# A chunkwise mLSTM and two feed-forward layers on one core: one merged state-update matmul, a sample chunk computed side by side, and five changes of order

## The chip, the cores and the metric

The kernel runs on one NeuronCore of a Trainium2 chip. Its engines are TensorE (PE in the profile; PEld is its weight load), VectorE (DVE), ScalarE (ACT), GpSimd (POOL) and SyncE (SP, which here issues nearly all DMAs). The metric is the device time of one execution in microseconds; "the time" of a kernel is the median of its runs.

## The reference, cut to what matters

The program is one inference step of a two-layer encoder for a prompt of 1024 frames and a sample of 32 frames, all in float32. Layer 0 is an mLSTM mixer, layer 1 a sliding-window attention with sinks; each is followed by a SwiGLU feed-forward part, and every sub-layer by `x <- LayerNorm(alpha * x + sublayer(x))`. So there are four LayerNorms; the kernel numbers them li = 0 (after the mLSTM), 1 (after the first feed-forward part), 2 (after the attention) and 3 (after the second).

The part that the change touches most is the recurrence over chunks of the mLSTM, per head with key size 64 and value size 128:

```
def mlstm_chunk(q, k, v, ig, lf, C0, n0, m0):
    b = jnp.cumsum(lf, axis=-1)
    log_d = where(causal, b[..., :, None] - b[..., None, :] + ig[..., None, :], -inf)
    inter = b + m0[..., None]
    m = jnp.maximum(inter, jnp.max(log_d, -1))
    d = jnp.exp(log_d - m[..., None])
    w_inter = jnp.exp(inter - m)
    qk = jnp.einsum('bhtd,bhsd->bhts', q, k) * d
    num = w_inter[..., None] * jnp.einsum('bhtd,bhde->bhte', q, C0) + jnp.einsum('bhts,bhse->bhte', qk, v)
    den = w_inter * jnp.einsum('bhtd,bhd->bht', q, n0) + jnp.sum(qk, -1)
    h = num / jnp.maximum(jnp.abs(den), jnp.exp(-m))[..., None]
    w_end = jnp.exp(b[..., -1:] - b + ig - m_new[..., None])
    C_new = decay[..., None, None] * C0 + jnp.einsum('bhs,bhsd,bhse->bhde', w_end, k, v)
    n_new = decay[..., None] * n0 + jnp.einsum('bhs,bhsd->bhd', w_end, k)
    return h, C_new, n_new, m_new
```

The final states `C` and `n` of the prompt and of the sample are outputs.

## The kernel before, in words

Activations lie transposed, features on the partitions and 1056 columns of time (1024 prompt, 32 sample). Dense products are made of three matmuls per 128 features of the contraction: each float32 operand is split into a high part in a reduced-precision float32 format and a low remainder, and `gemm` (lines 346 to 361; its matmuls are L358, L359, L360) adds high times high, high times low and low times high. Weights arrive by DMA (L157) and are split by ScalarE (the high part, L198) and by GpSimd or VectorE (the low part, L200).

Order is written out by hand. The dense products are the main thread; everything else is a Python generator in a `Weave`, and after each step of a product `wv.tick(us)` lets the generators whose pause is over emit their next instructions. A `yield 0.8` is thus a pause of 0.8 us of TensorE's dense work. `wv.drain(task)` emits the rest of a task at once. Every engine carries out its own instructions in the order in which they were emitted.

The stages on which the change bears:

- The mixer's projections, per pair of heads j (four pairs): `proj_q`, `proj_k` (heads on the output partitions) and `proj_v` (time on the output partitions, nine chunks of time: eight of 128 and the sample's of 32). For j = 0 `proj_v` makes the 16 gate columns too.
- `gate_task` and `gates(g)`: for three groups of columns, the gate arithmetic on 8 partitions; `gate_columns` transposes the result to time on the partitions (L786) and copies it to SBUF (L787). At the end one small product (L798) gives the decay of every chunk. It must be done before `begin()`, which starts the recurrence.
- `mlstm`: 36 visits (j, c), four pairs of heads by nine chunks, in five stages, one visit apart: `fetch` (DMAs of the decay rows, L824 and L828), `pre` (GpSimd, L839 to L846, and the exponentials L849 on ScalarE), `scores` (L856, L858), `values` (L872 to L916) and `place` (L923 to L925). In `values`, line 877 makes the state update of the two heads: two matmuls with 64 columns of weights each, one to PSUM partitions 0 to 63, one to 64 to 127. Line 890 adds it to the decayed state. After the last chunk of the prompt (c = 7) and after the sample's (c = 8) the state goes out by two DMAs, L897 and L898, the latter of one column of 128 values.
- `mixer_out` and the second half of `ffn` run over four quarters of 264 columns. After each quarter `norm_tail` launches an `ln_task`: a matmul with a constant matrix gives the mean (L417), VectorE centres (L422), ScalarE squares (L424), VectorE and GpSimd add the squares up (L426, L429), a second matmul gives the variance (L433), and the rest normalises (L438 to L469). Its pauses are the tuple `LN_PACE`. The matmul L433 stands in TensorE's stream between the matmuls of the next dense product.
- `ffn` begins while the fourth quarter's `ln_task` still runs: the first two up-projection tiles are plain products (`up_plain`), for half c = 0 of the columns and then for c = 1, and beside each half `sums(c)` makes the sums and differences of operands (L1240 to L1259) that the later tiles (`up_tile`, a scheme with seven products in place of eight) read.

Of the kernel before, what the change touches and what calls it, by code (L numbers as in the profile page):

```python
# [10 lines left out]
F32R = mybir.dt.float32r  # L11
# [41 lines left out]
    ((4.0, 1.2, 1.0, 3.6, 1.0, 1.4, 0.9), (3.8, 0.7, 0.8, 4.2, 0.8, 1.4, 1.0)),  # L53
    ((4.2, 0.9, 1.1, 4.4, 1.0, 1.4, 0.8), (4.2, 0.7, 0.9, 4.2, 0.8, 1.4, 0.8)),
)

RUSH = (3.2, 0.8, 0.6, 2.8, 0.8, 1.0, 0.6)

# [180 lines left out]
def kernel(ctx: ExitStack, tc: tile.TileContext, A, O):  # L239
# [14 lines left out]
    def new(p, tag, shape, dt=F32, bufs=1):  # L254
        uid[0] += 1
        return p.tile(list(shape), dt, name=f"{tag}_{uid[0]}", tag=tag, bufs=bufs)
# [106 lines left out]
    def psbank():  # L363
        return new(psx[1][0], "d", [P, 512], F32, bufs=psx[1][1])
# [30 lines left out]

    QUARTERS = [(group(g), (g % 2, slice(0, N4))) for g in range(4)]

    def ln_task(z_, lps, grp, li, last, final):
        cols, (c, zs) = grp
        w = cols.stop - cols.start  # L400

        rush = final and grp is QUARTERS[2]
        y = RUSH if rush else LN_PACE[li & 1][last]
        acc = z_[:, 0:2, c, zs]
        sq = [acc] + [z_[:, 2 + 2 * i : 4 + 2 * i, c, zs] for i in range(3)]
        rs, r2 = z_[:, 8, c, zs], z_[:, 9, c, zs]
        n = KT // 2

        def z2(kk):
            return ACT[:, 2 * kk : 2 * kk + 2, cols]  # L410

        def s2(i, kk):
            return SX[:, i, 2 * kk : 2 * kk + 2, cols]

        yield y[0]
        pm = new(lps, "ln", [P, 512], bufs=3 if li & 1 else 2)[:, :w]
        nc.tensor.matmul(pm, onesm[:], acc[:, 0, :], start=True, stop=True)  # L417
        yield y[1]
        for s in range(n + 2):
            if s < n:  # L420

                nc.vector.tensor_sub(z2(s), pm.unsqueeze(1).broadcast_to([P, 2, w]), z2(s))  # L422
            if 1 <= s <= n:
                nc.scalar.activation(sq[s - 1], z2(s - 1), AF.Square)  # L424
            if s >= 3:
                (nc.gpsimd if rush or not (last or s & 1) else nc.vector).tensor_add(acc, acc, sq[s - 2])  # L426
            yield y[2]
        if not rush:
            nc.vector.tensor_add(acc[:, 0], acc[:, 0], acc[:, 1])  # L429
        yield y[3]  # L430
        pv = new(lps, "ln", [P, 512], bufs=3 if li & 1 else 2)[:, :w]
        for i in range(1 + rush):
            nc.tensor.matmul(pv, onesm[:], acc[:, i, :], start=(i == 0), stop=(i == rush))  # L433
        yield y[4]

        if not li & 1:
            nc.scalar.preload_act_table_set("natural_log_exp_and_others")
        nc.scalar.activation(rs, pv, AF.Ln, bias=eps_ln[:])  # L438
        nc.scalar.activation(rs, rs, AF.Exp, scale=-0.5)
        nc.scalar.activation(r2, rs, AF.Square, scale=0.5 ** 0.5)  # L440
        yield y[5]
        nc.vector.scalar_tensor_tensor(r2, pv, eps_ln[:], r2, op0=ALU.add, op1=ALU.mult)
        nc.vector.scalar_tensor_tensor(rs, r2, 1.5, rs, op0=ALU.subtract, op1=ALU.mult)
        for s in range(n + 3):
            if s < n:
                eng = nc.gpsimd if rush and s & 1 else nc.vector
                eng.tensor_mul(z2(s), z2(s), rs.unsqueeze(1).broadcast_to([P, 2, w]))  # L447
            kk = s - 1
            if 0 <= kk < n:
                for k in (2 * kk, 2 * kk + 1):  # L450
                    z, gk, bk = ACT[:, k, cols], lng[:, li, k : k + 1], lnb[:, li, k : k + 1]
                    if rush and k & 1:
                        nc.gpsimd.tensor_scalar(z, z, gk, bk, op0=ALU.mult, op1=ALU.add)
                    elif li & 1 and last and k & 1:
                        nc.vector.tensor_scalar(z, z, gk, bk, op0=ALU.mult, op1=ALU.add)
                    else:
                        nc.scalar.activation(z, z, AF.Identity, scale=gk, bias=bk)  # L457
            kk = s - 2
            if 0 <= kk < n:
                if final:  # L460
                    nc.sync.dma_start(O["y"][:, 2 * kk : 2 * kk + 2, cols], z2(kk))
                else:
                    nc.scalar.copy(s2(0, kk), z2(kk))
                    if li == 1:
                        nc.scalar.dma_start(scr[:, 2 * kk : 2 * kk + 2, cols], z2(kk))
            kk = s - 3
            if kk >= 0 and not final:
                eng = nc.gpsimd if kk & 1 else nc.vector
                eng.tensor_sub(s2(1, kk), z2(kk), s2(0, kk).bitcast(F32))  # L469
            yield y[6]  # L470
# [216 lines left out]
    def proj_v(j):  # L687

        ua, ub = U_V[j]
        parts = [W.get(ua), W.get(ub)]  # L690
        m = 256 if j else 256 + NG
        rhs = []
        for k in range(KT):
            hi, lo = parts[k // 4][k % 4 // 2]
            s = slice((k % 2) * m, (k % 2) * m + m)
            rhs.append((hi[:, s], lo[:, s]))
        for c, c0, L, g, off in CH:
            ps = psbank()[:L, :m]
            gemm(ps, [(sxh[k][g][:, off : off + L], sxl[k][g][:, off : off + L]) for k in range(KT)], rhs)
            nc.vector.tensor_copy(vt[j][:L, c, :, 0:DV], ps[:, :256].rearrange("p (h e) -> p h e", h=2))  # L700
            if j == 0:
                nc.vector.tensor_copy(gt[:L, c, :], ps[:, 256:])
            mst["v"] += 1
        W.done(ua)
        W.done(ub)

    def gates(g):
# [40 lines left out]
            )  # L748
        yield 1.0
        if late:  # L750
            gate_columns(*late.pop())
        gg = g3[0:8, :n]
        nc.vector.tensor_sub(gg, ig, b)
        nm = b
# [27 lines left out]
    def gate_columns(g, g3):  # L782
        for c, c0, L, cg, off in CH:
            if cg == g:
                pt = new(psa, "T", [P, 512], bufs=2)
                nc.tensor.transpose(pt[:L, :96], g3[:96, off : off + L], ident[:96, :96])  # L786
                nc.scalar.copy(cols[g][:L, c % 3, :], pt[:L, :96])  # L787

    def gate_task():
        for g in range(3):  # L790
            while mst["v"] < 3 * g + 3:
                yield 0.5
            yield from gates(g)
        yield 3.0
        gate_columns(*late.pop())
        pd = new(psa, "T", [P, 512], bufs=2)
        for j in range(PAIRS):
            nc.tensor.matmul(pd[:, 9 * j : 9 * j + 9], sel[:, j, :], dec[:], start=True, stop=True)  # L798
        nc.vector.tensor_copy(dcol[:], pd[:, : 9 * PAIRS].rearrange("p (j c) -> p j c", j=PAIRS))

    mst = {"ready": 0, "done": 0, "v": 0, "go": False}
    prev = None
# [8 lines left out]
    def mlstm(gap):  # L811
# [53 lines left out]
        def values(j, c):  # L865
# [5 lines left out]
            for h in range(2):  # L871
                nc.tensor.matmul(ph[:L, h, :], s["p"][:L, h, :L], vt[j][:L, c, h, :], start=True, stop=C is None)  # L872
                if C is not None:
                    nc.tensor.matmul(ph[:L, h, :], s["qw"][:, h, :L], C[:], start=False, stop=True)
            for h in range(2):
                r = slice(64 * h, 64 * h + 64)
                nc.tensor.matmul(pc[r, : DV + 1], s["k"][:L, h, :], vt[j][:L, c, h, :], start=True, stop=True)

            small = new(pa2, "small", [P, 5, 2], bufs=3)
            enm = cols[g][:L, c % 3, 64 + 2 * j : 66 + 2 * j]  # L880
# [3 lines left out]
            nc.vector.scalar_tensor_tensor(u, den, -1.0, u, op0=ALU.mult, op1=ALU.max)  # L884
            nc.vector.reciprocal(u, u)
            Cn = new(pa2, "Cn", [P, DV + 1], bufs=3)
            if C is None:
                nc.vector.tensor_copy(Cn[:], pc[:, : DV + 1])
            else:
                nc.vector.scalar_tensor_tensor(  # L890
                    Cn[:], C[:], dcol[:, j, c : c + 1], pc[:, : DV + 1], op0=ALU.mult, op1=ALU.add
                )
            if c < 7:
                state[j, c + 1] = Cn
            else:
                k = "p" if c == 7 else "s"
                nc.sync.dma_start(O[k + "_C"][2 * DK * j : 2 * DK * (j + 1), :], Cn[:, :DV])  # L897
                nc.sync.dma_start(O[k + "_n"][2 * DK * j : 2 * DK * (j + 1), :], Cn[:, DV : DV + 1])  # L898
            junk = new(pa2, "junk", [P, DV])
            for h in range(2):  # L900
                nc.scalar.activation(
# [16 lines left out]
        def place(j, c):  # L918
            _, c0, L, g, off = CH[c]
            s = S.pop((j, c))  # L920
            pt = new(psa, "T", [P, 512], bufs=2)
            for h in range(2):
                nc.tensor.transpose(pt[:, h * P : h * P + L], s["h"][:L, h, :], ident[:L, :L])  # L923
            nc.scalar.copy(act[2 * j][g][:, off : off + L], pt[:, :L])
            nc.vector.tensor_copy(act[2 * j + 1][g][:, off : off + L], pt[:, P : P + L])  # L925

        def first(j, c):
            if c == 0:
# [189 lines left out]
    def ffn(layer, li, tasks, lx, final):  # L1118
# [107 lines left out]
        def sums(c):  # L1226
# [4 lines left out]

            todo = [(o, k) for k in range(0, H, 2) for o in ("t3", "t2", "t4")] + [("t1", k) for k in range(0, H, 2)]
            bufs = [Z[:, i : i + 2, c, :] for i in (7, 9)]

            def halve(s, low):
                if 0 <= s < len(todo):
# [675 lines left out]
```

## Time and profile before

| | |
|---|---|
| median of 3 runs | 2274.51 us (2273.16 to 2274.54) |
| profiled execution, own time | 2275.5 us |
| its span, first to last instruction | 2273.4 us |
| mean granted TensorE clock | 0.990 |
| TensorE busy | 2202.4 us, 97% of the span |
| VectorE busy | 1473.6 us, 65% |
| ScalarE busy | 1014.6 us, 45% |
| GpSimd busy | 1131.4 us, 50% |

How to read it: a group row gives line, engine, operation, the tiles written and read, the shapes and the count, then the busy time, the mean duration of one in ns, and the idle time of the engine just before them with what ended it. Matmuls overlap one another, so the duration of one (some 0.28 us) is not what it costs; the cost is the distance from its start to the next start. A float32 matmul without the split shows as two instructions. A row of waits gives the waiting instruction, the work that it waited for, the total in us, the number of times and the longest. A timeline row gives start and duration, and in brackets the engine's idle time just before and what ended it. A row of windows gives, for a stretch of time, each engine's busy time and instructions and the granted clock of TensorE (PEclk, 1.00 is full).

### The profile page before, as it was taken

How to read it: one execution, taken by the hardware profiler on the slowest of the kernel's cores; microseconds unless marked ns; L12 is line 12 of the kernel's file. 1: busy time of each engine (PE TensorE's matmuls, PEld its weight loads, DVE VectorE, ACT ScalarE, POOL GpSimd, SP SyncE). 2: the span in 40 equal slices, each digit the busy share in tenths (PEclk: the TensorE clock that was granted, in tenths of full speed). 3: DMA queues.
4: the chain of work that ended last, by engine and by line, in shares of the span. 5: the costliest groups of instructions: out<-in, count | busy, mean ns of one | idle time of the engine just before them, and what ended most of it. 6: DMA issues, size and time to landing. Idle time of an engine off the chain costs nothing. (4 is left out here: it accounts for less than half of the span.)

```text
span 2273.4 us, 44324 instructions
## 1 busy us (share of the span) xinstructions
PE 2202.4 (97%) x17190; PEld 2158.1 (95%) x17190; DVE 1473.6 (65%) x2771; ACT 1014.6 (45%) x2281; POOL 1131.4 (50%) x1040
## 2 busy tenths in 40 slices
PE   9999999999999999999998999989999999999997
PEld 9889989999999999999998998889999999999997
DVE  4354466777666665466667788877666666466657
ACT  4343354455444444322246788756444444432124
POOL 2443333226666665554326676633666666554422
PEclk9999999999999999999999999999999999999999
DMA  4222112301444444697424211311343344397712
GB/s 147 70 56 62 46 42 74 115 28 67 147 148 152 152 140 145 214 331 235 163 78 137 85 59 44 125 65 56 114 151 134 142 152 154 125 336 259 247 57 77
DMA packets 167394, 291.54 MB, mean 128 GB/s; under 512 B 16592, under 2 KB 123144, under 8 KB 167184
## 3 DMA queue, kind: packets, MB, share of 16 engines
q1 hardware_dynamic: 162832, 284.38, 37.1%
q10 hardware_dynamic: 4352, 4.33, 0.5%
q8 instruction: 135, 2.21, 0.4%
q14 instruction: 75, 0.61, 0.1%
HBM read 203.89 MB, written 82.94 MB: 126 GB/s over the span
## 5 line engine op out<-in xcount | busy, mean ns | idle before, releaser
L200 POOL TENSOR_TENSOR wl_s<-wr,wh_s 128x512 fp32r<-128x512 f32 x224 | 316.2, 1431 | 238.5 <-ACT wh_s L198 163.3
L358 PE MATMUL d<-sx,wh 128*128 128x264 f32 (+2 forms) x1068 | 342.4, 321 | 0.7 <-DVE act L1471 0.7
L360 PE MATMUL d<-sx,wl 128*128 128x264 f32 (+2 forms) x1068 | 328.4, 308 | 3.0 <-DVE wl L200 2.1
L359 PE MATMUL d<-sx,wh 128*128 128x264 f32 (+2 forms) x1068 | 328.1, 307 | 0.5 <-DVE sx L389 0.3
L198 ACT CAST wh_s<-wr 128x512 fp32r<-128x512 f32 x224 | 135.5, 617 | 317.4 <-DVE wr L175 286.4
L358 PE MATMUL A<-sx,wh_s 128*128 128x264 f32 x896 | 254.6, 284 | 2.2 <-ACT z L1304 2.2
L359 PE MATMUL A<-sx,wh_s 128*128 128x264 f32 x896 | 254.2, 284 | 0.0
L360 PE MATMUL A<-sx,wl_s 128*128 128x264 f32 x896 | 254.0, 283 | 0.0
L200 POOL TENSOR_TENSOR wl<-wr,wh 128x512 fp32r<-128x512 f32 (+2 forms) x103 | 141.5, 1380 | 220.1 <-ACT wh L198 191.4
L358 PEld LDWEIGHTS d<-sx,wh 128*128 128x128 f32 x1068 | 204.7, 192 | 5.0 <-issue 1.7
L360 PEld LDWEIGHTS d<-sx,wl 128*128 128x128 f32 x1068 | 204.2, 191 | 4.3 <-DVE wl L200 2.8
L359 PEld LDWEIGHTS d<-sx,wh 128*128 128x128 f32 x1068 | 204.9, 192 | 1.6 <-DVE sx L389 0.6
L200 POOL TENSOR_TENSOR wl_a<-wr,wh_a 128x512 fp32r<-128x512 f32 x112 | 170.2, 1526 | 51.8 <-ACT wh_a L198 42.7
L358 PE MATMUL d<-sx,ex 128*128 128x264 f32 x624 | 182.1, 292 | 0.8 <-ACT sx L388 0.8
L360 PE MATMUL d<-sx,ex 128*128 128x264 f32 x624 | 178.7, 286 | 4.0 <-DVE ex L200 4.0
L359 PE MATMUL d<-sx,ex 128*128 128x264 f32 x624 | 178.5, 286 | 0.6 <-DVE sx L389 0.5
L358 PEld LDWEIGHTS A<-sx,wh_s 128*128 128x128 f32 x896 | 168.4, 188 | 2.7 <-ACT z L1304 2.7
L360 PEld LDWEIGHTS A<-sx,wl_s 128*128 128x128 f32 x896 | 168.8, 188 | 0.0
L359 PEld LDWEIGHTS A<-sx,wh_s 128*128 128x128 f32 x896 | 168.4, 188 | 0.0
L1176 POOL TENSOR_TENSOR z<-z 128x528 fp32r<-128x528 f32 x76 | 105.1, 1382 | 106.0 <-issue 52.9
L1659 POOL TENSOR_SCALAR s<-s,st 128x256 f32<-128x256 f32 (+1 forms) x144 | 123.9, 872 | 57.2 <-DVE st L1657 47.5
L1175 ACT CAST z<-z 128x528 fp32r<-128x528 f32 x136 | 85.9, 631 | 95.8 <-DVE z L1188 46.9
(326 smaller groups left out, 7387.2 us busy)
## 6 DMA issues: line engine op xcount, KB each, us to landing
wr<-in_gu SPq DMA_DIRECT2D x96, 512.0 KB
hs_x<-z SPq DMA_DIRECT2D x72, 528.0 KB
hs_t<-z SPq DMA_DIRECT2D x64, 528.0 KB
sx<-hs_x SPq DMA_DIRECT2D x112, 264.0 KB
sx<-hs_t SPq DMA_DIRECT2D x64, 264.0 KB
ex<-hs_t SPq DMA_DIRECT2D x64, 264.0 KB
wr<-in_dn SPq DMA_DIRECT2D x32, 512.0 KB
ex<-hs_x SPq DMA_DIRECT2D x32, 264.0 KB
```

The lines of the kernel that those rows point to most:

```text
L198: self.nc.scalar.copy(hi, r)
L200: eng.tensor_sub(lo, r, hi.bitcast(F32))
L358: nc.tensor.matmul(out, ah, bh, start=start and k == 0, stop=False, **kw)
L359: nc.tensor.matmul(out, ah, bl, start=False, stop=False, **kw)
L360: nc.tensor.matmul(out, al, bh, start=False, stop=stop and k == last, **kw)
L1175: nc.scalar.copy(hi.bitcast(F32R), buf(s))
L1176: eng.tensor_sub(lo.bitcast(F32R), buf(s), hi)
L1659: nc.gpsimd.tensor_scalar_mul(p[:R, h, lo:256], p[:R, h, lo:256], st[:R, 2, h : h + 1])
```

## The change

1. In `values` the two state-update matmuls of 64 weight columns become one with all 128 columns, which streams both heads' values (258 columns). The two blocks off the diagonal of the result are not used, so line 890's VectorE instruction becomes two, one on each half of the partitions.
2. In `proj_v` the sample chunk's high and low parts stand side by side as 64 weight columns (`xs`, copied once by GpSimd). Two matmuls per 128 features do the work of three; ScalarE copies the lower half of the result (`vlow`) and VectorE adds the halves.
3. The state outputs L897 and L898 are issued in `place`, one stage later than `values`.
4. `gate_columns` pauses for 0.8 us after each transpose; a gate group starts 1.0 us later, and the last transposes 1.4 us later.
5. `LN_LAG`: the first quarter's `ln_task` of LayerNorm 2 waits 7.0 us longer before its variance matmul.
6. `sums(c)` does not start until the fourth quarter's variance matmul has been emitted (the set `squared`).
7. The program is built with a smaller scratch area for dynamic DMAs (`dynamic_dma_scratch_size=2048`).

```
+LN_LAG = {(2, 0): 7.0}
...
-        yield y[3]
+        yield y[3] + LN_LAG.get((li, cols.start // N4), 0.0)
         pv = new(lps, "ln", [P, 512], bufs=3 if li & 1 else 2)[:, :w]
         for i in range(1 + rush):
             nc.tensor.matmul(pv, onesm[:], acc[:, i, :], start=(i == 0), stop=(i == rush))
+        squared.add((li, cols.start // N4))
         yield y[4]
...
-            ps = psbank()[:L, :m]
-            gemm(ps, [(sxh[k][g][:, off : off + L], sxl[k][g][:, off : off + L]) for k in range(KT)], rhs)
...
+            if L < P:
+                ps = psbank()[: 2 * L, :m]
+                for k, (wh, wl) in enumerate(rhs):
+                    both = xs[:, k]
+                    nc.tensor.matmul(ps, both, wh, start=k == 0, stop=False)
+                    nc.tensor.matmul(ps, both, wl, start=False, stop=k == KT - 1)
+                    wv.tick(2 * (m / 2400.0 + 0.003))
+                low = new(pa, "vlow", [DEC, 256 + NG])[:, :m]
+                nc.scalar.copy(low, ps[L:])
...
+                    nc.vector.tensor_add(out, a, b)
...
                 nc.scalar.copy(cols[g][:L, c % 3, :], pt[:L, :96])
+                yield 0.8
...
+            yield 1.0
             yield from gates(g)
-        yield 3.0
-        gate_columns(*late.pop())
+        yield 4.4
+        yield from gate_columns(*late.pop())
...
+    xs = pa.tile([P, KT, 2 * DEC], F32R, name="xs")
+    for i in range(2):
+        nc.gpsimd.tensor_copy(xs[:, :, i * DEC : (i + 1) * DEC], SX[:, i, :, SEQ:])
...
-            for h in range(2):
-                r = slice(64 * h, 64 * h + 64)
-                nc.tensor.matmul(pc[r, : DV + 1], s["k"][:L, h, :], vt[j][:L, c, h, :], start=True, stop=True)
+            keys = s["k"][:L].rearrange("p h d -> p (h d)")
+            nc.tensor.matmul(pc[:, : 2 * (DV + 1)], keys, vt[j][:L, c], start=True, stop=True)
...
+            for h in range(2):
+                r = slice(64 * h, 64 * h + 64)
+                own = pc[r, h * (DV + 1) : (h + 1) * (DV + 1)]
...
+                    nc.vector.scalar_tensor_tensor(
+                        Cn[r], C[r], dcol[r, j, c : c + 1], own, op0=ALU.mult, op1=ALU.add
+                    )
...
-                k = "p" if c == 7 else "s"
-                nc.sync.dma_start(O[k + "_C"][2 * DK * j : 2 * DK * (j + 1), :], Cn[:, :DV])
-                nc.sync.dma_start(O[k + "_n"][2 * DK * j : 2 * DK * (j + 1), :], Cn[:, DV : DV + 1])
+                s["out"] = Cn
...
+            if "out" in s:
+                k, Cn = "p" if c == 7 else "s", s["out"]
+                nc.sync.dma_start(O[k + "_C"][2 * DK * j : 2 * DK * (j + 1), :], Cn[:, :DV])
+                nc.sync.dma_start(O[k + "_n"][2 * DK * j : 2 * DK * (j + 1), :], Cn[:, DV : DV + 1])
...
+            while (li - 1, 3) not in squared:
+                yield 0.3
```

More of the change, by code (lines that the diff above doesn't have):

```diff
@@ L396 @@
     QUARTERS = [(group(g), (g % 2, slice(0, N4))) for g in range(4)]
+    squared = set()
     def ln_task(z_, lps, grp, li, last, final):
@@ L697, in proj_v @@
         for c, c0, L, g, off in CH:
-            ps = psbank()[:L, :m]
-            gemm(ps, [(sxh[k][g][:, off : off + L], sxl[k][g][:, off : off + L]) for k in range(KT)], rhs)
-            nc.vector.tensor_copy(vt[j][:L, c, :, 0:DV], ps[:, :256].rearrange("p (h e) -> p h e", h=2))
-            if j == 0:
-                nc.vector.tensor_copy(gt[:L, c, :], ps[:, 256:])
+            v = vt[j][:L, c, :, 0:DV]
+            if L < P:
[7 more added lines that the diff above has]
+                nc.scalar.copy(low, ps[L:])
+                parts = [(v, slice(0, 256))] + ([(gt[:L, c, :], slice(256, m))] if j == 0 else [])
+                for out, s in parts:
+                    a, b = (t[:, s] for t in (ps[:L], low))
+                    if out is v:
+                        a, b = (t.rearrange("p (h e) -> p h e", h=2) for t in (a, b))
+                    nc.vector.tensor_add(out, a, b)
+            else:
+                ps = psbank()[:L, :m]
+                gemm(ps, [(sxh[k][g][:, off : off + L], sxl[k][g][:, off : off + L]) for k in range(KT)], rhs)
+                nc.vector.tensor_copy(v, ps[:, :256].rearrange("p (h e) -> p h e", h=2))
+                if j == 0:
+                    nc.vector.tensor_copy(gt[:L, c, :], ps[:, 256:])
             mst["v"] += 1
@@ L792, in gate_task @@
                 yield 0.5
+            yield 1.0
             yield from gates(g)
-        yield 3.0
-        gate_columns(*late.pop())
+        yield 4.4
+        yield from gate_columns(*late.pop())
         pd = new(psa, "T", [P, 512], bufs=2)
@@ L886, in values @@
             Cn = new(pa2, "Cn", [P, DV + 1], bufs=3)
[L887 to L892, printed above, removed]
+            for h in range(2):
+                r = slice(64 * h, 64 * h + 64)
+                own = pc[r, h * (DV + 1) : (h + 1) * (DV + 1)]
+                if C is None:
+                    nc.vector.tensor_copy(Cn[r], own)
+                else:
+                    nc.vector.scalar_tensor_tensor(
+                        Cn[r], C[r], dcol[r, j, c : c + 1], own, op0=ALU.mult, op1=ALU.add
+                    )
             if c < 7:
@@ L1881 @@
     from concourse.bass_utils import run_bass_kernel_spmd
-    nc = bacc.Bacc("TRN2", target_bir_lowering=False, num_devices=1)
+    nc = bacc.Bacc("TRN2", target_bir_lowering=False, num_devices=1, dynamic_dma_scratch_size=2048)
     arrays = {f"in_{n}": v for n, v in _arrays(inputs).items()}
```

## The prediction

> **What bounds the kernel now.** I read the page first, then TensorE's waits, then windows around the longest of them, then the timelines at the lines that the change touches.
>
> ```profile
> span 2273.4 us, 44324 instructions
> PE 2202.4 (97%) x17190; PEld 2158.1 (95%) x17190; DVE 1473.6 (65%) x2771; ACT 1014.6 (45%) x2281; POOL 1131.4 (50%) x1040
> ```
>
> TensorE is busy for 97% of the span, so there are two kinds of gain: less work on TensorE, which shows in full, and shorter waits of TensorE, of which there are 71 us in all. The waits that the change addresses are these:
>
> ```profile
> PE ln L433 <- DVE z L429: 13.6, 5, 5.8
> PE T L877 <- DVE act L925: 2.8, 3, 1.9
> PE T L786 <- ACT cols L787: 1.5, 3, 1.0
> PE T L786 <- ACT g L771: 0.3, 1, 0.3
> ```
>
> A wait costs more than itself where the granted clock falls after it:
>
> ```profile
> 74.00:81.00 7.00, 7.00 (x30) 6.97 (x30) 0.20 (x1) 1.31 (x3) 0.31 (x1) 0.51 0.00 0
> 81.00:97.00 16.00, 16.00 (x114) 16.00 (x113) 2.00 (x4) 2.39 (x5) 7.79 (x8) 1.00 0.28 82
> 517.70:521.10 3.40, 3.40 (x18) 3.40 (x17) 3.37 (x3) 3.29 (x7) 2.21 (x2) 0.50 0.29 77
> 521.10:524.50 3.40, 3.40 (x29) 3.40 (x29) 3.22 (x7) 3.08 (x6) 0.00 (x0) 0.99 0.20 80
> 1490.50:1497.40 6.90, 3.15 (x12) 2.94 (x13) 4.60 (x6) 2.00 (x4) 2.81 (x2) 0.51 0.36 90
> ```
>
> TensorE is busy in the first row, yet it issues 30 instructions in 7 us where the next row has 114 in 16 us, that is 50 in 7 us: 20 too few at 0.14 us are 2.8 us. By the same count the third row loses 11 at 0.12, 1.3 us, and the fifth, in its 3.15 busy us, some 13 at 0.12, 1.5 us.
>
> **A. One state-update matmul.** A visit of the recurrence, and a full-width float32 product of 256 columns (L856) for comparison:
>
> ```profile
> 153.84 0.59 PE L856 MATMUL S<-qz,kT 128*128 128x256 f32 x2
> 154.26 0.27 PE L858 MATMUL T<-ident,kT 128*128 128x128 f32 x1
> 156.40 0.39 PE L872 MATMUL H<-vt,p 128*128 128x129 f32 x2
> 156.62 0.39 PE L874 MATMUL H<-Cn,qwz 128*128 128x129 f32 x2
> 156.94 0.44 PE L877 MATMUL T<-vt,ks 128*64 128x129 f32 x4
> 157.31 0.45 PE L358 MATMUL d<-sx,oh 128*128 128x384 f32 x1
> 157.60 0.34 PE L359 MATMUL d<-sx,oh 128*128 128x384 f32 x1
> 157.77 0.34 PE L360 MATMUL d<-sx,oh 128*128 128x384 f32 x1
> ```
>
> From start to start one 129-column product costs 0.22 us (156.40 to 156.62), so L874 would be done at 156.84, but L877 starts at 156.94; its four instructions take 0.37; the next dense matmul takes 0.29 in place of 0.17 (157.60 to 157.77). So the update costs 0.10 + 0.37 + 0.12 = 0.59 us, of which 0.22 lies in the change to 64 columns and back. One product of 258 columns costs what L856 does, 0.42 to 0.43 (153.84 to 154.26). Gain 0.14 to 0.16; 36 visits at 0.14 are 5.0 us. I take 4.7, since a few visits wait anyway.
> [...]
>
> VectorE's added half (36 instructions) falls into a wait:
>
> ```profile
> L890 DVE SCALAR_TENSOR_TENSOR Cn<-Cn,dcol,T 128x129 f32<-128x129 f32 x28 | 9.4, 335 | 0.0
> L908 DVE TENSOR_SCALAR small<-small 128x2 f32<-128x2 f32 x32 | 8.0, 248 | 40.6 <-ACT junk L901 40.6
> ```
>
> It is 0.33 us, emitted just before L908, which waits 40.6/32 = 1.3 us for ScalarE. Nothing on the path; without that cover it would be 12 us of VectorE.
>
> **B. The sample's values.** Three matmuls take 0.37 us:
>
> ```profile
> 58.74 0.29 PE L358 MATMUL d<-wh,sx 128*32 128x272 f32 x1
> 59.11 0.29 PE L358 MATMUL d<-wh,sx 128*32 128x272 f32 x1
> ```
>
> One of three goes, for eight k and four pairs: 32 x 0.12 = 3.8 us. The added ScalarE copies and VectorE adds come after the product and delay only a bank that is used two products later (GpSimd's two copies of `xs` are priced in D). I put 0.7 us for all of this together, since a VectorE that waits for ScalarE delays what is behind it; the bounds are 0 and 2. The smaller DMA scratch I put at nothing: every DMA of the page's queues is issued by SP or ScalarE, none by GpSimd.
>
> **C. Gate transposes.**
>
> ```profile
> 71.50 0.25 PE L786 MATMUL T<-ident,g 96*128 96x96 f32 x1
> 73.36 0.26 PE L786 MATMUL T<-ident,g 96*32 96x96 f32 x1 [1.03 <-ACT cols L787]
> L856 PE MATMUL S<-qz,kT x72: 219/378/455, 97.7 to 321.3; 128*128 128x256 f32 x64, 128*32 128x64 f32 x8
> ```
>
> The third transpose waits for the copy of the first, behind ScalarE's exponentials. With pauses of 0.8 us and a start 1.4 later those are done: the two rows of L786 in the list of waits (1.5 + 0.3 = 1.8 us) go, and with them the slow clock at 74, 2.8 us: 4.6. The added pauses (1.0, 2.4, 1.4, 2.4) delay the end of the gates from 75 to some 82, and the recurrence first issues at 97.7, so `begin()` doesn't catch them.
> [...]
>
> **D. State outputs.**
>
> ```profile
> SPq L897 <- DVE Cn L890: 33.8, 8, 8.3
> 134.65 0.43 SPq L898 DMA_DIRECT2D out_p_n<-Cn  x1
> 135.61 1.12 SPq L828 DMA_DIRECT2D wib<-scrw  x2
> 143.10 0.45 POOL L845 TENSOR_TENSOR qwz<-qT,wib 64x128 f32<-64x128 f32 x1 [7.66 <-PE T L877]
> 149.45 0.44 PE L877 MATMUL T<-vt,ks 128*64 128x129 f32 x4 [1.95 <-DVE act L925]
> ```
>
> SP stands 33.8 us before the outputs, and the decay rows of later visits are queued behind. At the change of pair, rows fetched at 135.61 right behind the output are used by GpSimd only at 143.10, after 7.66 idle; the exponentials on ScalarE wait for that, and TensorE then waits 1.95 at 149.45. Issued in `place`, the outputs go behind the next fetch, so the row needed next is early; the one after it is late instead, but with a visit of time. Gain 1.9, bounds 0 and 2.8 (all of L877's waits). GpSimd's copies of `xs`, 256 elements each, are at most two of the row at 143.10 each, 0.9 us, 1.8 in all: the 2 us of B if nothing covers them.
>
> **E. The lag in LayerNorm 2.**
>
> ```profile
> 1492.11 1.74 DVE L200 TENSOR_TENSOR ex<-wr,ex 128x512 fp32r<-128x512 f32 x1
> 1493.78 0.42 DVE L429 TENSOR_TENSOR z<-z 128x264 f32<-128x264 f32 x1
> 1494.25 1.25 PE L433 MATMUL ln<-z,onesm 128*128 128x264 f32 x2 [5.82 <-DVE z L429]
> 1497.88 0.43 DVE L1103 SCALAR_TENSOR_TENSOR act<-act,d 128x264 f32<-128x264 f32 x1 [2.75 <-PE d L360]
> ```
>
> TensorE comes to L433 at 1488.4 (1494.25 - 5.82). Seven us later, at 1495.4, L429 is done. The wait of 5.82 and the slow clock, 1.5, go: 7.3. What is late next: VectorE takes up the result of the product around L433 at 1497.88, as soon as it ends; without the 7.3 it ends at 1490.5, and the next one comes to its second half, twelve matmuls at 0.12 later, at 1492.0, while VectorE splits the weights for it until 1493.85, whatever TensorE does. That returns 1.9, and I add half a slow clock, 0.8. The rest of the normalisation moves 7 us on, against the next quarter's centring on VectorE and ScalarE; for that I put 1.4, half the mean wait at L433 (13.6/5). Net 3.2, bounds 0 and 7.3.
>
> **F. Sums behind the fourth quarter.**
>
> ```profile
> 511.46 1.80 DVE L1240 TENSOR_TENSOR ex<-z,ex 128x528 fp32r<-128x528 f32 x1
> 516.47 0.71 PE L433 MATMUL ln<-z,onesm 128*128 128x264 f32 x2 [2.87 <-DVE z L429]
> 516.40:540.00 23.60, 23.53 (x179) 23.47 (x180) 17.80 (x25) 18.66 (x35) 12.37 (x9) 0.93 0.20 68
> 541.41 0.39 PE L360 MATMUL d<-sx,wl 128*128 128x264 f32 x1 [0.58 <-DVE wl L200]
> 1570.06 0.71 PE L433 MATMUL ln<-z,onesm 128*128 128x264 f32 x2 [2.85 <-DVE z L429]
> ```
>
> The sums (the first row is one of their instructions) come before the squares on VectorE. Behind them, the waits 2.87 and 2.85 and the slow clock at 517.7 (1.3) go: 7.0. But the sums then meet the second half's, and VectorE has 23.6 - 17.8 = 5.8 us free there, for at least the 1.80 moved in and the 4.2 (2.87 + 1.3) that TensorE no longer loses. That is 6.0 for 5.8, and the wait of 0.58 for split weights shows that there is no slack for single instructions. I let each layer give back 1.5. Net 4.0, bounds 0 and 7.0.
>
> **Sum.** 4.7 + 3.8 + 4.6 + 1.9 + 3.2 + 4.0 - 0.7 = 21.5 us. The profiled execution took 2275.5 by itself, which is 1.0 over the median of 2274.5; so 2254 for such an execution, and 2253 for the median.
>
> **Rivals.**
> 1. VectorE gives everything back: E and F return nothing, since the same VectorE work stands behind the same products. For it: the split at 1493.85 and the 0.58 at 541.41. Against it: VectorE idles 5.8 us in the window. 2253 + 7.2 = 2260.
> 2. Nothing is given back: E 7.3 and F 7.0. 2253 - (4.1 + 3.0) = 2246.
> [...]
> 4. Slower: the outputs, now behind another fetch, delay rows that are needed at once. Six outputs have visits behind them (c = 7 and 8 of three pairs), each with up to the 7.66 that GpSimd waited. The other parts gain 19.6, so it decides from (19.6 + 4.5)/6 = 4.0 us each reaching TensorE; at 5 us each, 2274.5 - 19.6 + 30 = 2285. Against it: one such wait now gives TensorE 1.95.
> 5. No change: new waits eat it all, 2274.
>
> **How the numbers follow.** Chances: the sum as forecast 0.52 (its own range 2248 to 2259), rival 1 0.22, rival 2 0.12, rival 3 0.04, rival 4 0.05, rival 5 0.05. The range 2244 to 2266 holds all but the last two; its upper end is A, B and the 1.8 of C alone, less 2 for the additions: 2274.5 - 8.3 = 2266. About 0.2% can be told from no change, 4.5 us, so faster means under 2270. Faster 0.90, within 0.05, slower 0.05.
>
> **What would show it.** A: one group of the state update with 128 columns and 258 values, x72, and 0.43 from its start to the next. B: 16 dense matmuls with 64 columns per pair. C: no wait at the transposes, clock 1.00 at 74. D: L897 waiting for nothing, no gap near 149. E: no gap at the first L433 of LayerNorm 2, one of some 2 us for `ex` L200 behind it. F: no gap at the fourth L433, longer waits for `wl` L200 some 25 us on. The prediction is wrong if slow-clock windows stand at new places, if the waits of TensorE in the recurrence grow, or if the up-projections wait for VectorE for over 3 us each.

## The result, and the profile after

The changed kernel takes 2266.48 us (median of 16 runs, 2261.86 to 2272.89) against 2274.53 (16 runs beside them, 2272.20 to 2278.97). The ratio is 0.9966, 95% interval 0.9957 to 0.9974: 8.05 us less, where 21.5 were forecast. The profiled execution took 2261.86 and is the shortest of its 16, at a mean granted clock of 0.996 where the 16 have 0.993 on the mean; it is 4.6 below the median. So its trace is read here for places more than for sums.

First the page of the changed kernel, then those of TensorE's waits in it on which the change bears: what it waited for, us in all, times, longest. The change adds two lines to the helpers: L358 to L360 are now L360 to L362, L198 and L200 are L200 and L202, L433 is L437, L877 is L904, L786 is L808, L925 is L953.

```profile
span 2259.8 us, 44187 instructions
PE 2189.0 (97%) x17086; PEld 2149.0 (95%) x17086; DVE 1490.3 (66%) x2807; ACT 1015.3 (45%) x2285; POOL 1135.6 (50%) x1042
...
PE d L362 <- DVE wl L202: 6.0, 6, 1.7
PE d L362 <- DVE ex L202: 4.9, 6, 2.0
PE A L360 <- ACT z L1338: 3.3, 2, 1.7
PE T L904 <- DVE act L953: 3.0, 5, 1.8
PE d L361 <- DVE sx L474: 2.6, 2, 1.3
PE d L361 <- POOL sx L474: 1.0, 2, 0.5
```

The three waits that E and F address (5.8, 2.9, 2.9 of the 13.6 at the old L433) are gone, and so are the transposes'. In their place stand waits for split weights (`wl`, 2.1 before), for split activations (`sx` L474, 0.2 in all before) and for `ex` (4.0 before).

Where the time goes is seen when the same TensorE instruction is looked up in both traces. By how much it starts earlier in the changed kernel, in us; the last column is the kernel before against its own second profile, which is told of below:

| place in the trace of before | changed kernel | before again |
|---|---|---|
| 96, the gates are done | 5.1 | 3.1 |
| 345, the recurrence is done | 10.9 | 3.8 |
| 420, output projection | 9.8 | 3.8 |
| 520, behind the fourth quarter's squares, first up-projection | 13.9 | 3.6 |
| 600, same up-projection | 6.2 | 3.3 |
| 1466, attention is done | 10.8 | 4.1 |
| 1506, behind the first squares of LayerNorm 2 | 16.0 | 4.2 |
| 1572, behind the fourth squares | 19.2 | 2.6 |
| 1647, second up-projection | 12.9 | 3.4 |
| 2248 | 13.6 | 3.9 |

A to D give 9.8, E gives 5.2, and each time F first gives 3 to 4 and then takes 6 to 8: F costs 3.6 (9.8 to 6.2) and 3.1 (16.0 to 12.9). The 4.6 between 600 and 1466 (6.2 to 10.8) are from no part of the change. TensorE idles as long there as before (23.8 and 22.9 us), but it works at half clock for 3.2 us there in this profile and for 15.1 us in that of before.

### The profile page after: what moved, and what is told of

It reads as the page before. It is cut to its first block, busy times and chain, and to the rows that moved or that the text cites. A ratio compares the mean times of both kernels' runs of the same rounds, so it can differ in the third digit from the quotient of the medians.

```text
span 2259.8 us, 44187 instructions
## 1 busy us (share of the span) xinstructions
PE 2189.0 (97%) x17086; PEld 2149.0 (95%) x17086; DVE 1490.3 (66%) x2807; ACT 1015.3 (45%) x2285; POOL 1135.6 (50%) x1042
## 5 line engine op out<-in xcount | busy, mean ns | idle before, releaser
L202 POOL TENSOR_TENSOR wl_s<-wr,wh_s 128x512 fp32r<-128x512 f32 x224 | 316.8, 1435 | 241.3 <-ACT wh_s L200 158.2
L360 PE MATMUL d<-sx,wh 128*128 128x264 f32 (+2 forms) x1068 | 340.2, 319 | 1.2 <-DVE act L1505 0.7
L362 PE MATMUL d<-sx,wl 128*128 128x264 f32 (+2 forms) x1068 | 325.6, 305 | 8.4 <-DVE wl L202 6.0
L200 ACT CAST wh_s<-wr 128x512 fp32r<-128x512 f32 x224 | 135.5, 617 | 316.6 <-DVE wr L177 289.2
L360 PE MATMUL A<-sx,wh_s 128*128 128x264 f32 x896 | 254.6, 284 | 3.3 <-ACT z L1338 3.3
L202 POOL TENSOR_TENSOR wl<-wr,wh 128x512 fp32r<-128x512 f32 (+2 forms) x103 | 141.4, 1379 | 231.7 <-ACT wh L200 200.6
L362 PE MATMUL A<-sx,wl_s 128*128 128x264 f32 x896 | 254.0, 283 | 0.0
L362 PEld LDWEIGHTS d<-sx,wl 128*128 128x128 f32 x1068 | 200.9, 188 | 10.8 <-DVE wl L202 7.6
L361 PEld LDWEIGHTS d<-sx,wh 128*128 128x128 f32 x1068 | 201.6, 189 | 5.8 <-DVE sx L474 3.1
L360 PEld LDWEIGHTS d<-sx,wh 128*128 128x128 f32 x1068 | 201.7, 189 | 5.1 <-ACT z L443 1.1
L202 POOL TENSOR_TENSOR wl_a<-wr,wh_a 128x512 fp32r<-128x512 f32 x112 | 169.4, 1520 | 49.0 <-ACT wh_a L200 42.2
L362 PE MATMUL d<-sx,ex 128*128 128x264 f32 x624 | 178.5, 286 | 5.0 <-DVE ex L202 4.9
L360 PE MATMUL d<-sx,ex 128*128 128x264 f32 x624 | 181.0, 290 | 0.8 <-ACT sx L390 0.8
L360 PEld LDWEIGHTS A<-sx,wh_s 128*128 128x128 f32 x896 | 168.4, 188 | 3.7 <-ACT z L1338 3.7
L362 PEld LDWEIGHTS A<-sx,wl_s 128*128 128x128 f32 x896 | 168.9, 188 | 0.0
```

Of the source, the lines that this page charges most:

```text
L200: self.nc.scalar.copy(hi, r)
L202: eng.tensor_sub(lo, r, hi.bitcast(F32))
L360: nc.tensor.matmul(out, ah, bh, start=start and k == 0, stop=False, **kw)
L361: nc.tensor.matmul(out, ah, bl, start=False, stop=False, **kw)
L362: nc.tensor.matmul(out, al, bh, start=False, stop=stop and k == last, **kw)
```

## Experiments

Below, the hold is part F (the sums wait for the squares), and the lag is part E. Ratios are to the kernel before, timed on the same chip beside each; us are ratios times 2274.5, against before.

| kernel | ratio (95%) | us |
|---|---|---|
| the change | 0.9966 (0.9957 to 0.9974) | -7.7 |
| e1, no hold | 0.9943 (0.9930 to 0.9957) | -13.0 |
| e2, no lag | 0.9986 (0.9977 to 0.9995) | -3.2 |
| e3, lag for hold | 0.9968 (0.9956 to 0.9981) | -7.3 |
| e4, sample visits split | 0.9966 (0.9953 to 0.9978) | -7.7 |
| e5, hold, lows on GpSimd | 1.0020 (1.0011 to 1.0029) | +4.5 |
| e6, no hold, lows on GpSimd | 1.0004 (0.9994 to 1.0014) | +0.9 |
| e7, merge alone | 1.0002 (0.9993 to 1.0011) | +0.5 |
| e8, late hold | 0.9947 (0.9933 to 0.9960) | -12.1 |
| e9, hold, copies on ScalarE | 0.9926 (0.9913 to 0.9940) | -16.8 |
| e10, no hold, sample split | 0.9955 (0.9942 to 0.9968) | -10.2 |
| e11, two holds | 0.9946 (0.9932 to 0.9960) | -12.3 |

### The hold and the lag, taken away

e1 takes F away:

```diff
-            while (li - 1, 3) not in squared:
-                yield 0.3
```

> The changed kernel without F: the sums do not wait for the fourth quarter's squares. Theory (the hold stacks both halves' sums on VectorE, which is then busy 14.9 of 15 us for two stretches in the first up-projection and hands its lateness to TensorE; by the two traces the hold cost 3.6 us there and 3.1 in the second): faster than the changed kernel by 6 to 7, about 2260; the waits of 2.9 at the fourth L433 (here L437) come back, and those for sx L474, wl L202 and z L1338 behind it go. Rival 1 (the forecast's step: the hold is worth 4.0): slower, about 2270. Rival 2 (the hold is a wash, and what is missing from the forecast is lost to half-clock stretches elsewhere): within 1.5 of 2266.

It is 5.3 us faster than the changed kernel (0.9943 against 0.9966), so F costs, and about what the traces say. TensorE's waits in the first up-projection, from the fourth quarter's squares on; first the changed kernel, then e1:

```profile
PE d L362 <- DVE wl L202: 3.0, 3, 1.7
PE A L360 <- ACT z L1338: 1.7, 1, 1.7
PE d L361 <- DVE sx L474: 1.3, 1, 1.3
PE A L360 <- ACT z L1321: 0.8, 1, 0.8
PE d L361 <- POOL sx L474: 0.5, 1, 0.5
PE A L362 <- POOL wl_s L202: 0.2, 1, 0.2
```

```profile
PE ln L437 <- DVE z L433: 2.9, 1, 2.9
PE A L360 <- ACT z L1336: 2.6, 1, 2.6
PE d L362 <- DVE wl L202: 0.2, 1, 0.2
```

The hold exchanges one wait of 2.9 for five kinds that sum to 5.8 (3.0 + 1.3 + 0.8 + 0.5 + 0.2). The wait for `z` in L1338 (L1336, L1304), called the store's wait below, stands in every kernel: ScalarE's copy that frees the bank stands there behind a cast, and the cast waits for a store. Its length is left out of the sums, as it changes without the kernel too: 0.9 and 1.4 in the two profiles of before. ScalarE's rows show it for before and then for e1, with TensorE waiting 0.9 and 2.6 behind them:

```profile
588.30 0.63 ACT L1175 CAST z<-z 128x528 fp32r<-128x528 f32 x1 [3.53 <-DMA hs_t<-z]
```

```profile
579.94 0.63 ACT L1207 CAST z<-z 128x528 fp32r<-128x528 f32 x1 [5.23 <-DMA hs_t<-z]
```

e2 takes E away:

```diff
-LN_LAG = {(2, 0): 7.0}
+LN_LAG = {}
```

> The changed kernel without E: no lag in LayerNorm 2. By the aligned traces the lag was worth 5.2 us: 2271.5, with a wait of 5 to 6 at the first L437 of LayerNorm 2. By the forecast's step it was worth 3.2: 2269.5. By the forecast's rival 1 (all given back): 2266.5.

0.9986 against 0.9966: E is worth 4.5 us, between the 5.2 of the traces and the 3.2 of the forecast; with the two intervals it may be 3 us more or less. In e2 the wait at L437 is there again, 5.24 at 1487.34, with a half clock behind it (0.22 us from one dense product to the next from 1488.60 on, where the changed kernel has 0.12 from 1483.03 on); what is left of it in the changed kernel is the wait for `ex`:

```profile
1482.81 0.39 PE L362 MATMUL d<-sx,ex 128*128 128x264 f32 x1 [2.01 <-DVE ex L202]
```

### Can F's wait be had by the means of E?

```diff
-LN_LAG = {(2, 0): 7.0}
+LN_LAG = {(2, 0): 7.0, (0, 3): 3.0, (2, 3): 3.0}
...
-            while (li - 1, 3) not in squared:
-                yield 0.3
```

> The hold of F replaced by a lag of 3.0 us before the squares' matmul of the fourth quarter in LayerNorms 0 and 2, the same means as E. Theory (the waits of 2.9 can go if VectorE's order stays and only TensorE's instruction moves): both waits gone and no stacked sums, 2260 less 2 x (2.0 to 4.0), so 2252 to 2256. Rival (whatever is taken from that wait comes back as lateness of VectorE a quarter later, since the normalisation's tail moves 3 us towards the second half's first product): 2260, as without the hold, with waits for sx L474 of about 3 in place of those at L437.

The rival was right, and mildly put: 0.9968, 5.7 us worse than e1, which has neither the hold nor these two lags. The wait at L437 is gone, and 5.2 us stand behind it (without the store's 2.6):

```profile
PE d L362 <- DVE wl L202: 2.6, 2, 2.4
PE d L361 <- POOL sx L474: 1.2, 2, 1.0
PE d L360 <- ACT sx L468: 1.0, 1, 1.0
PE d L361 <- DVE sx L474: 0.4, 1, 0.4
```

So removing the wait does not pay there by itself. At the first quarter of LayerNorm 2 (E) it does: behind that one, VectorE is late for one `ex`, and then in time again. In the 30 us from 1479 on, where this happens in the changed kernel, VectorE is free for 7.7 us.

### Is it VectorE?

Rows of stretches: us, then busy us and instructions of TensorE, its loads, VectorE, ScalarE and GpSimd, then the clock. Before, from the squares on:

```profile
516.00:531.00 15.00, 14.53 (x105) 14.47 (x106) 11.78 (x18) 14.20 (x26) 6.58 (x5) 0.89 0.22 72
531.00:546.00 15.00, 14.42 (x118) 14.21 (x118) 12.39 (x15) 6.68 (x14) 8.32 (x6) 1.00 0.21 72
```

The changed kernel:

```profile
506.00:521.00 15.00, 13.20 (x107) 12.78 (x106) 10.53 (x14) 12.53 (x24) 6.79 (x5) 1.00 0.14 42
521.00:536.00 15.00, 13.57 (x108) 12.97 (x107) 14.93 (x15) 6.89 (x13) 10.66 (x7) 1.00 0.19 71
536.00:551.00 15.00, 12.20 (x94) 11.38 (x93) 14.76 (x18) 6.08 (x12) 8.89 (x6) 1.00 0.10 36
```

VectorE has 4.5 us free in the first stretch, where the sums were, and none for the next 30. Two experiments take VectorE's half of the sums' low parts away from it. e5 gives them to GpSimd, e6 does so without the hold:

```diff
-    (nc.vector if s & 1 else nc.gpsimd).tensor_sub(d[:, 1], bufs[s % 2], d[:, 0].bitcast(F32))
+    nc.gpsimd.tensor_sub(d[:, 1], bufs[s % 2], d[:, 0].bitcast(F32))
```

> The changed kernel, hold kept, with all the subtractions of the sums' low parts on GpSimd in place of every second one on VectorE. Theory (the hold costs because VectorE, busy 14.9 of 15 us in two stretches, is the bound of the first up-projection): VectorE loses some eight instructions of 0.7 to 1.8 us there, the waits of TensorE in that stretch (7.7 us in all) fall by half or more in each layer, and the kernel is 4 to 7 us faster than the changed one: about 0.994 of the kernel before. Rival (the hold costs because the sums themselves are late, or ScalarE's part of them): the waits stay or move to GpSimd's instructions, 0.9966 or slower.

> The changed kernel without the hold, and with all the subtractions of the sums' low parts on GpSimd. Theory (the wait at the fourth quarter's squares is VectorE's queue, and is shortened by taking work off VectorE, not by reordering it): the waits of 2.9 and 3.0 at L437 fall under 1.5 each, nothing comes back, 3 to 6 us faster than without the hold alone (0.9943): about 0.992. Rival (another chain, of ScalarE and the quarter's own steps, sets the time of the squares): the waits stay near 2.9, 0.994.

Both came out on the rivals' side and beyond: 12 and 14 us slower than the same kernels without it (1.0020 - 0.9966, 1.0004 - 0.9943). Longer waits in the two up-projections make up some 5 and 8 us of that in the traces; where the rest lies is not shown. In e6 the wait for the squares even grew:

```profile
PE ln L437 <- DVE z L433: 3.7, 1, 3.7
PE d L362 <- DVE wl L202: 2.7, 1, 2.7
```

So "VectorE alone is the bound" falls: taking work off it did not help, since its other instructions took longer instead. In e5 22.3 us of low parts are gone from VectorE, but its other 2791 instructions sum to 1595.9 us where the changed kernel has 1577.1, 18.8 more; in e6 18.6 us are gone and 12.9 come back (1589.8 against 1576.9 in e1). e9 gives the same instructions to ScalarE, as copies:

```diff
+    if s & 1:
+        nc.scalar.copy(d[:, 1], bufs[s % 2])
+    else:
+        nc.gpsimd.tensor_sub(d[:, 1], bufs[s % 2], d[:, 0].bitcast(F32))
-    (nc.vector if s & 1 else nc.gpsimd).tensor_sub(d[:, 1], bufs[s % 2], d[:, 0].bitcast(F32))
```

> The changed kernel, hold kept, with VectorE's half of the subtractions of the sums' low parts replaced by copies on ScalarE, which has room there (it is busy 6 to 9 of 15 us). The values of those low parts are left out of the computation: they are the sums themselves, not what is left of them; the number of instructions stays. Theory (with the hold, both halves' sums run at once, VectorE and GpSimd work at the same time, and an instruction that takes 0.70 alone takes 1.6 to 1.8 beside the other): VectorE's work falls by some 11 us in each of the two up-projections, the waits there (7.7 in the first) fall under 3.5 each, and the kernel gets 6 to 9 us faster than the changed one: 0.993 or less. Rival (the sums come late through the hold itself, whatever VectorE has to do): the waits stay over 6 each, 0.9966.

0.9926: 9.1 us faster than the changed kernel, as the theory said. VectorE's other instructions grow by 6.9 us only, and beside the store's wait only 1.8 us of waits are left in the first up-projection:

```profile
PE A L360 <- ACT z L1341: 2.0, 1, 2.0
PE d L361 <- DVE sx L474: 1.3, 1, 1.3
PE d L361 <- POOL sx L474: 0.5, 1, 0.5
```

What is short there is VectorE and GpSimd together. An instruction of VectorE on two operands of 512 or 528 columns (`TENSOR_TENSOR`) takes 0.68 to 0.71 us in all 541 cases of before in which GpSimd does nothing at the time; of the 220 that take over 1.0 us, 218 overlap GpSimd's work for more than half of their time. Twelve of the sixteen low parts that VectorE makes for the sums show what stacking does to them, before and after:

```profile
L1240 DVE TENSOR_TENSOR ex<-z,ex 128x528 fp32r<-128x528 f32 x12 | 12.9, 1073 | 0.0
```

```profile
L1274 DVE TENSOR_TENSOR ex<-z,ex 128x528 fp32r<-128x528 f32 x12 | 16.6, 1386 | 0.0
```

Beside GpSimd the same instruction takes up to 1.91 us, and moving the low parts from VectorE to GpSimd lost 12 and 14 us (e5, e6). Why the two slow each other is not shown.

### How long a hold?

e8 starts the sums at once and lets only their fourth step wait for the squares, e11 also lets the fifth wait for the quarter's end:

```diff
-            while (li - 1, 3) not in squared:
-                yield 0.3
...
             for s in range(len(todo) + 2):
+                while s == 3 and (li - 1, 3) not in squared:
+                    yield 0.3
+                while s == 4 and tasks[3] in wv.tasks:      # e11 alone
+                    yield 0.3
```

> The changed kernel with the hold of F moved from the start of the sums to their fourth step, so that only the instructions right ahead of the fourth quarter's squares stand back (some 3 us later instead of 11). Theory (VectorE and GpSimd together have a fixed amount of work between the fourth quarter and the second up-projection tile, and TensorE waits for the end of it, wherever the wait stands): the waits of 2.9 at L437 go and come back behind it as waits for sx, wl or banks; the time is that without the hold, 0.9943 within 0.001. Rival (the order decides: the hold lost because it was too long): the waits go, under 1.5 us per layer come back, 0.992 or less.

> The late hold, and a second one behind it: the first half's sums go on from their fifth step only when the fourth quarter's normalisation is issued, since in the late hold GpSimd's third low part (L1272, 1.83 us) stands ahead of the quarter's own (L474) and TensorE waits 1.76 for that. So the sums stand back some 7 us, between the late hold (3 us, 0.9947) and the hold of the change (11 us, 0.9966). Theory (the amount of work of VectorE and GpSimd counts, and stacking makes it dearer): the 1.76 goes, waits for wl or banks of 1.5 to 3 take its place in each up-projection, and the time lies between: 0.995 to 0.997. Rival (order is what counts): the 1.76 goes twice and nothing comes: 0.993.

0.9947 and 0.9946: as without a hold. The waits only change their names, e8 first:

```profile
PE d L361 <- POOL sx L474: 1.8, 1, 1.8
PE A L360 <- ACT z L1338: 1.6, 1, 1.6
PE ln L437 <- DVE z L433: 1.1, 1, 1.1
PE d L362 <- DVE wl L202: 0.9, 1, 0.9
```

```profile
PE d L360 <- DVE z L1253: 1.8, 1, 1.8
PE A L360 <- ACT z L1340: 1.8, 1, 1.8
PE ln L437 <- DVE z L433: 1.2, 1, 1.2
PE d L360 <- ACT wh L200: 0.3, 1, 0.3
PE d L362 <- DVE wl L202: 0.2, 1, 0.2
```

Without the store's wait TensorE stands 3.5 us in before (2.9 + 0.6), 3.1 in e1, 3.8 in e8, 3.5 in e11, 5.8 with the full hold, 5.2 with the lag, 1.8 in e9. As far as these runs show, up to some 7 us of hold the amount of work decides and not its order; at 11 us the stacking makes the work dearer (the low parts' 1073 and 1386 ns above). In e11 the 1.76 went and 1.8 for a bank came, as its theory said; the time lies just under the theory's 0.995.

### The merge

e7 is the kernel before with part A alone, and the kernel before was profiled a second time:

> The kernel before with part A alone, the merged state update. By the visits' rows in the changed kernel (0.13 gained on 32 visits, 0.26 lost on four): 3 us less work on TensorE; what of it stays depends on the waits behind, so 2273 to 2276 where before has 2276. By the forecast's step: 4.7, 2271. [...]

> The kernel before, unchanged, profiled once more. If half-clock stretches fall where TensorE has waited, those of 2.7 at the transposes (near 75) and of 1.6 to 1.7 at the fourth quarter's squares (near 517) stand there again. If they fall by chance of time, they stand at other places. The waits themselves stand where they were within 0.2 us each, except those that end on a transfer.

e7: 1.0002, no change; the interval runs from 1.6 us faster to 2.5 slower. The visit's rows are as forecast. In the changed kernel, below, it is 1.01 us from the last product (L902) to the third dense one (142.29 to 143.30), and in e7 too (154.83 to 155.84); before has 1.15 (156.62 to 157.77), so 0.14 are gained.

```profile
142.29 0.39 PE L902 MATMUL H<-Cn,qwz 128*128 128x129 f32 x2
142.51 0.60 PE L904 MATMUL T<-vt,ks 128*128 128x258 f32 x2
...
143.30 0.34 PE L362 MATMUL d<-sx,oh 128*128 128x384 f32 x1
```

But looked up instruction by instruction, e7 gains nothing on before from 101 to 161 us, 1.7 from there to 302, and loses 0.2 by 342. The 1.7 are what the 17 full visits there gain, less what the two of the sample lose (17 x 0.13 - 2 x 0.26). In the first pair's visits TensorE waits for the chain of `p`, `ks` and `act` anyway, and the change of pair waits as before (2.01 against 1.95).

And the four visits of the sample, with 32 rows, are slower merged. e4 splits these alone:

```diff
+            if L < P:
+                for h in range(2):
+                    r = slice(64 * h, 64 * h + 64)
+                    own = pc[r, h * (DV + 1) : (h + 1) * (DV + 1)]
+                    nc.tensor.matmul(own, s["k"][:L, h, :], vt[j][:L, c, h, :], start=True, stop=True)
+            else:
+                keys = ...
```

> The changed kernel with the state update of the four sample visits (c = 8, 32 rows) split into two matmuls again, the other 32 visits merged. Theory (the merge gains 0.13 on each of the 32 full visits and loses 0.26 on each of the four sample visits, so 2.9 in all in place of the 4.7 forecast): the four visits go back from about 0.83 to 0.57 from their start to the regular beat, 1.0 us in all, 2265.4. Rival (the longer sample visits are not from the merged form): they stay at 0.8, 2266.5. The time alone hardly tells this apart; the rows of the visits do.

The same visit in the changed kernel and in e4:

```profile
195.17 0.70 PE L904 MATMUL T<-vt,ks 32*128 32x258 f32 x2
195.79 0.39 PE L360 MATMUL d<-wh,sx 128*128 128x256 f32 x1
```

```profile
193.98 0.43 PE L907 MATMUL T<-vt,ks 32*64 32x129 f32 x4
194.34 0.39 PE L360 MATMUL d<-wh,sx 128*128 128x256 f32 x1
```

0.62 against 0.36 from its start to the next product: 0.26 lost, four times. The rows bear the theory out, and from 161 to 302, with two of the four visits, e4 is 0.56 faster than the changed kernel; the time (0.9966) cannot tell 1.0 us. Why 32 rows by 128 columns take so long is open. e10 joins the split with the missing hold:

> The changed kernel without the hold, and with the sample visits' state update split: what the runs so far say is best. 0.9943 for the first, and 1.0 us (0.0005) for the second, if no wait takes it: 0.9938. Rival (the microsecond on the four visits is taken by the waits behind them): 0.9943 as without the hold alone.

0.9955, with an interval that holds 0.9943 and 0.9966: nothing is shown by it. Of the versions that compute the same, none is shown to beat e1; e8 and e11 are level with it, and all three beat the change.

The second profile of before repeats the waits of the first: 2.87 and 2.83 at the fourth L433, 5.53 at the first of LayerNorm 2, 0.58 for `wl`. Its half clocks differ: it has one behind the fourth squares of LayerNorm 2 (at 1565.1), which the first has not, and it lacks the one behind the transposes. Its 7 us there:

```profile
69.50:76.50 7.00, 5.65 (x40) 5.13 (x39) 0.19 (x1) 3.96 (x12) 1.67 (x4) 1.00 0.17 66
```

## Why the prediction was wrong

The forecast was 2253, 13.5 below the result. Its terms, and what they came to (us gained):

| term | forecast | measured |
|---|---|---|
| A | 4.7 | 1.5 (1.7 - 0.2 in e7) |
| B | 3.8 | 4.0 (32 matmuls at 0.124) |
| C | 4.6 | 3.2 (1.8, and 2.7 in one of two profiles) |
| D | 1.9 | 1.5 |
| E | 3.2 | 4.5 |
| F | 4.0 | -5.3 |
| additions | -0.7 | -0.8 |
| not foreseen | | -1.1 |
| sum | 21.5 | 7.5, to 8.05 measured |

E and F are differences of two ratios and may each be off by 3 to 4 us, and the rest is read from single traces. That the sum comes within 0.6 of the result is partly luck.

**F is the step that failed**: a gain of 4.0 was forecast and a loss of 5.3 measured, 9.3 of the 13.5. It said that VectorE "has 23.6 - 17.8 = 5.8 us free there, for at least the 1.80 moved in". That the wait goes was right, with longer waits for `wl` behind it. But 1.80 was one of five instructions that move; the others of before stood in its trace too (503.96 and 506.09 likewise, 0.71 each, L1255 and L1257):

```profile
502.12 1.81 DVE L1253 TENSOR_TENSOR z<-act 128x528 f32<-128x528 f32 x1
...
513.30 1.69 DVE L1253 TENSOR_TENSOR z<-act 128x528 f32<-128x528 f32 x1
```

With the 1.80 that is 6.7 us. The 4.2 that TensorE no longer loses come on top, so VectorE has 10.9 to do in 5.8: 5.1 too much, which is more than the 4.2 gained. The durations then grew as well, since the work met GpSimd's: VectorE's sixteen low parts took 22.3 us in place of 18.5. The forecast's own sign of being wrong came too, waits of the up-projections for VectorE of over 3 us each: they are 4.3 (3.0 + 1.3) in the first and 4.8 in the second. The forecast's rival 1 (VectorE gives everything back) had the place and the mechanism, but it ended at zero and took E and F as one case; F went below zero, and E stands.

**A** failed on "36 visits at 0.14": a gain of TensorE's work counts only in visits that do not wait, and four of the 36 are of another shape. In those four alone the merge does not pay (0.62 against 0.36).

**B** was right. The sample's products are two rows a k in place of three (L708 and L709, 64 columns, 58.18 and 58.31), as forecast. The additions cost a wait of 0.61 for `wl` at 63.87 and the slower first products behind it, some 0.8.

**C**: both waits are gone, as said. The half clock was counted in full from one profile; the second has the same waits (1.04 the longest) without it. A third, e7's, whose gates are those of before, has a half clock half as long there (3.4 us in place of 6.8), and takes 1.5 us more than the second from 50 to 96 where the first takes 3.0 more. So it was worth about half. The same wait does and doesn't end in a half clock: in the first profile the granted clock behind 1.03 is 0.51 (74 to 81), in the second it is 1.00 from 69.5 to 76.5 and on to 92.5.

**D** was right in what it gains, 0.42 in place of 1.95 at the change of pair. One of its signs did not come: SP still waits at the outputs (L956, L897 before), 19.3 us where it was 33.8.

```profile
SPq L956 <- DVE Cn L920: 19.3, 7, 6.1
```

But the decay rows are no longer late behind that. GpSimd idles 48.3 us before the instructions that read them (L873), at most 5.3 at a time; before has 71.0 and at most 10.1 (L845), and e7, which lacks D, 70.9. Rival 4 (late rows) did not come. TensorE's waits at L904 do not fall in all (3.0, 2.8 before): 1.77 stand at the end of the recurrence (317.5), where before has no wait at L877 but 2.8 at the transposes of that last stretch (L923, now L951 with 0.3).

**E**: the returned wait for `ex` is 2.01, forecast 1.9; the 1.4 put for the moved rest of the normalisation did not show, which is about the difference of 1.3.

**Not foreseen**: at the start of the output projection TensorE comes 10.9 earlier, VectorE's chain of the output's normalisation only 9.8, so 1.51 stand where 0.46 stood:

```profile
389.77 0.39 PE L361 MATMUL d<-sx,ex 128*128 128x264 f32 x1 [1.51 <-DVE sx L391]
```

## What to carry to other kernels

When work is moved past a wait, list every instruction that passes it, by the trace, and set their sum against the idle time of the stretch that receives them; then ask which engine works beside them there. A wait that ends on VectorE is worth removing if VectorE has idle time behind it (E, 7.7 us free in 30), and worth nothing if it has none (F, 0.3 free in 30 with the hold), however the wait is removed (e3, e8, e11). A gain on TensorE's own work counts only where TensorE is not already waiting for a chain, so count the visits, not the loop.

## What was not expected of the hardware

- VectorE and GpSimd slow each other: VectorE's `TENSOR_TENSOR` of 528 columns takes 0.70 us alone and up to 1.9 beside, GpSimd's low part 1.32 alone (514.59 in the changed kernel) and 1.79 beside (521.23); with VectorE's half of the low parts on GpSimd the kernel lost 12 to 14 us.
- A float32 product of 32 rows, 128 columns of weights and 258 values takes 0.62 us to the next product; two of 32 rows by 64 columns with 129 values take 0.36.
- The half clock is partly chance. Behind the fourth quarter's squares, a wait of 2.8 to 3.0 stands ten times in the profiles of before (two of them), e7, e1 and e10; TensorE's clock is halved behind eight of them, for 3.4 or 6.8 us. Among the 16 runs of the changed kernel the one with the lowest mean clock, 0.990, took 2270.6, and the one with the highest, 0.996, 2261.9.
